# A hybrid mLSTM / short-conv block on one core: two convolutions put off into the down projection, and another split of the plain tail

## The chip, the cores and the metric

The kernel runs on one core of one Trainium2 chip. The metric is device microseconds of one execution; a time shown for a kernel is the median of its runs. PE is TensorE (the matmuls), DVE is VectorE, ACT is ScalarE, POOL is GpSimd, SP is SyncE. A name with q (ACTq, SPq) is that engine's queue of instructions that start a DMA.

## The reference, cut to what matters

512 tokens of width 2048 pass through two mixers and a gated MLP. Only the MLP and the last norm are touched:

```python
hn = rmsnorm(h, norm_ffn_g)
u = causal_dwconv(hn @ w_up, ffn_conv_w, ffn_conv_b)     # 2048 -> 2 * 5504, 3 taps over the tokens
gate, val = jnp.split(u, 2, axis=-1)
h = h + (jax.nn.silu(gate) * val) @ w_down               # 5504 -> 2048
return rmsnorm(h, norm_out_g)
```

## The kernel before, in words

Activations lie transposed: channels on the partitions, the 512 tokens on the free axis. All projections are cut into **items**. An item makes two blocks of 128 output channels for all tokens; it is worked through in **steps**, each of 512 input channels. A step has two **cells** of 21 matmuls (128x128 weights, 256 tokens): 7 products of sums of blocks in place of 8 plain ones, each as three matmuls, weight high x activation high (L281), high x low (L282), low x high (L283). For that, each step's weights are loaded into `raw` by SP (L252, L253, L262), two blocks in it are added to by accumulating DMAs of POOL (L255), sums are made by DVE (L218, L223), ACT rounds `raw` into `wh` (L233, once for each cell) and DVE takes the rest into `wl` (L237, once for each cell). There are 6 `raw`, 4 `wh` and 3 `wl` buffers. The activations of a step are made once for a phase by the same means (L344 to L354, L358, L361).

Items alternate between two sets of three PSUM banks. One of the seven products goes to a bank that both sets share (`bank_83` in the order, `P_BANK` in the code), half of it for each set; it comes first in the last cell of an item and last in every other cell. When an item's last step is issued, ACT copies its half of the shared bank into the item's buffer `z` (L305, `evac_first`), and in the next step DVE adds the other banks to it (L311 to L314, `evac_ops`). In the first and the last two items of a phase the steps of the two items alternate.

What is left to do for an item is its **post**: a list of pieces, kept in the queue `posts`, of which at most one piece each of the first two entries is issued at the end of a step. A piece is issued while `credit` (DVE time left over, counted by the program) allows it; otherwise it waits until the steps left to `due(num)` are no more than its pieces. `flush(n)` issues at once whatever posts are left up to item n. A store or add that a piece asks for is issued in the step after it (`late`).

- Up item j (items 64 to 106; `up_post`): normalise `z` (L688, DVE); two scaled copies by ACT into a buffer, mA or mB in turn (L853, L854); two taps each on DVE (L857, L858 and L861, L862); SiLU (L865, ACT); the product (L868, DVE); the store to `a_d`, which ACT issues (L150).
- Down item (items 107 to 130, three chunks of K of 8 items each; `down_post`): ACT negates half of `z` (L879), POOL adds `z` to `h_d` in DRAM by an accumulating DMA of 512 KB (L157). Chunk 0 has 3 steps to an item. Items 107 and 108 fill steps 0 to 5 of the down projection, item 109 ends at step 8, 110 at 11, 111 at 14, 112 at 17, and 113 and 114 fill steps 18 to 23.

The z of a down item is the next of a ring of five buffers (`DOWN_Z`). Before, 107 to 112 take z_93, z_92, z_91, mA, mB and again z_93, where z_93, z_92 and z_91 were the z of the up items 104, 105 and 106.

Three of the 43 input blocks of the down projection are left for the **plain part** at the end: 16 steps (n = 0 to 15; token half 0 for n below 8), 18 matmuls each (L1202 to L1204). After step n, DVE adds the partial `h` to the bank (L1215, `last_post`), ACT squares it (L1216), DVE adds the square to its half's sum (L1220, `last_acc`). A matmul with a constant sums over the partitions (L1225, `last_sum`), ACT takes the root (L1232, `last_root`), DVE makes the row that scales (L1233 to L1235). Then each (half, block pair) is scaled and written to the output: where ACT had multiplied it by the weights of the norm (L1241, `last_gain`), by one DVE product (L1248), else by two DVE operations that take in the weights (L1252); ACT issues the output DMA (L1254). SP loads the partial `h` three steps ahead (L1186, `hf_load`). Of half 0, pairs 4 to 7 have their weights from ACT, of half 1 all.

The lines that order this around the change, in the main loop:

```python
flush(it.num - 3)
evac_first(it)
...
for x in list(posts)[:2]:
    cost, fn = x[1][0]
    if not rush and cost and credit <= cost / 2 and len(x[1]) < due(x[0]) - s:
        break
    x[1].popleft()
    credit -= cost
    fn()
```

## Time and profile before

| what | value |
|---|---|
| median of 3 runs | 2601.21 us (2599.85 to 2602.29) |
| the profiled execution, its own time | 2603.19 us |
| its span, first to last instruction | 2601.5 us |
| PE busy in the span | 2548.2 us, 98% |
| DVE, ACT, POOL busy | 2123.1, 1316.3, 862.5 us |
| mean granted clock of TensorE | 0.993 of full speed |

The profiled execution's own time is 2.0 us above the median, and its span 1.7 us below its own time. Times of day below ("at 2147.64") count from the start of the span. A granted clock of 1.00 is the level of 2.4 GHz, 0.50 that of 1.2 GHz; a value between is a mean over a stretch that had both. In a timeline a row is one instruction: start, length, engine, line, operation, output<-inputs, and in brackets the idle time before it with what ended it.

### The profile page before, as it was taken

The page shows a single profiled execution, that of the slowest core. Times are in us where ns is not written, and L with a number is a line of the kernel's source. Part 1 is how long each engine was busy: PE and PEld are TensorE (multiplying, and loading weights), DVE is VectorE, ACT ScalarE, POOL GpSimd, SP SyncE. Part 2 cuts the span into 40 slices and gives each one's busy share as a digit, 9 for nine tenths or more (in the row PEclk, how much of TensorE's full clock was granted, in tenths as well). Part 3 has the DMA queues.
Part 4 walks back from the last instruction along what each step waited for, and adds up shares of the span by engine and source line. Part 5 has one row for each costly group of instructions (what it writes and reads, how often), then busy time and mean ns, then how long its engine had stood idle before and what let it go on. Part 6 is the DMA issues. An engine that isn't in the chain of part 4 may idle for free.

```text
span 2601.5 us, 55134 instructions
## 1 busy us (share of the span) xinstructions
PE 2548.2 (98%) x20886; PEld 2528.9 (97%) x20886; DVE 2123.1 (82%) x3239; ACT 1316.3 (51%) x1731; POOL 862.5 (33%) x996
## 2 busy tenths in 40 slices
PE   9999999999999999999899999999999999999997
PEld 8999999999999999999899999999999999999997
DVE  8687778886777888967889888888888898879766
ACT  7454554546556544445554544454444554545444
POOL 3343333333333212232333333333333323353430
PEclk9999999999999999999999999999999999999998
DMA  9799889898998899999989988898989889999995
GB/s 256 176 238 241 234 225 253 221 256 217 231 253 221 233 297 235 267 271 245 234 220 227 224 224 218 222 224 223 223 221 224 223 223 234 249 273 252 270 228 169
DMA packets 479003, 609.83 MB, mean 234 GB/s; under 512 B 44640, under 2 KB 309856, under 8 KB 478736
## 3 DMA queue, kind: packets, MB, share of 16 engines
q1 hardware_dynamic: 307280, 423.46, 51.5%
q0 software_dynamic: 144224, 137.67, 35.2%
q10 hardware_dynamic: 27232, 45.17, 4.8%
q8 instruction: 163, 2.67, 0.4%
q14 instruction: 104, 0.85, 0.1%
HBM read 541.65 MB, written 60.82 MB: 232 GB/s over the span
## 4 chain that ended last, share of the span: by engine, by line
PE 65%; DVE 5%; DMA 3%; issue 2%; ACT 0%; POOL 0%; DVEq 0%; SPq 0%; ACTq 0%; POOLq 0%
PE bank L283 21%; PE bank L282 21%; PE bank L281 21%; DVE act L361 1%; DVE wl L237 1%; DMA raw<-in_w_out_dram 1%; DMA raw<-in_w_up_dram 1%; DVE raw L218 0%; DMA xraw<-mc_d 0%; DMA xraw<-a_d 0%; DVE xraw L344 0%; PE bank L639 0%; DMA mc_d<-z 0%; PE bank L1204 0%; PE bank L1203 0%
## 5 line engine op out<-in xcount | busy, mean ns | idle before, releaser
L283 PE MATMUL bank<-act,wl 128*128 128x256 f32 x6712 | 1906.1, 284 | 24.3 <-DVE wl L237 23.7
L281 PE MATMUL bank<-act,wh 128*128 128x256 f32 x6712 | 1914.0, 285 | 4.9 <-ACT z L305 2.1
L282 PE MATMUL bank<-act,wh 128*128 128x256 f32 x6712 | 1903.2, 284 | 2.1 <-DVE act L361 2.1
L233 ACT ACTIVATE wh<-raw 128x896 fp32r<-128x896 f32 x904 | 858.2, 953 | 1076.1 <-PE bank L282 719.0
L283 PEld LDWEIGHTS bank<-act,wl 128*128 128x128 f32 x6712 | 1292.2, 193 | 29.2 <-DVE wl L237 29.1
L281 PEld LDWEIGHTS bank<-act,wh 128*128 128x128 f32 x6712 | 1292.2, 193 | 8.5 <-DVE z L311 2.4
L282 PEld LDWEIGHTS bank<-act,wh 128*128 128x128 f32 x6712 | 1292.2, 193 | 5.4 <-DVE act L361 2.5
L237 DVE TENSOR_TENSOR wl<-raw,wh 128x896 fp32r<-128x896 f32 x904 | 982.7, 1088 | 372.2 <-PE bank L283 244.2
L255 POOL DMA_DIRECT2D raw<-in_w_up_dram x344 | 299.2, 952 | 578.7 <-DMA raw<-in_w_up_dram 243.8
L255 POOL DMA_DIRECT2D raw<-in_w_dram x284 | 247.1, 944 | 505.2 <-DMA raw<-in_w_dram 320.9
L255 POOL DMA_DIRECT2D raw<-in_w_down_dram x160 | 141.5, 1002 | 253.0 <-DMA raw<-in_w_down_dram 144.2
L218 DVE TENSOR_TENSOR raw<-raw 128x256 f32<-128x256 f32 x452 | 189.8, 420 | 11.4 <-DMA raw<-in_w_up_dram 5.1
L223 DVE TENSOR_TENSOR raw<-raw 128x256 f32<-128x256 f32 x452 | 189.6, 420 | 0.3
L358 ACT ACTIVATE act<-xraw 128x1792 fp32r<-128x1792 f32 (+1 forms) x52 | 86.9, 1672 | 63.1 <-DVE xraw L354 61.1
L361 DVE TENSOR_TENSOR act<-xraw,act 128x1792 fp32r<-128x1792 f32 (+1 forms) x52 | 103.4, 1988 | 0.0
L688 DVE TENSOR_TENSOR z<-z,rstd 128x1024 f32<-128x1024 f32 x83 | 101.1, 1219 | 0.0
L311 DVE TENSOR_TENSOR z<-bank,z 128x512 f32<-128x512 f32 x122 | 83.6, 685 | 16.2 <-ACT z L305 12.6
L312 DVE TENSOR_TENSOR z<-bank,z 128x512 f32<-128x512 f32 x122 | 83.5, 684 | 0.8
L314 DVE TENSOR_TENSOR z<-bank,z 128x512 f32<-128x512 f32 x122 | 83.4, 684 | 0.0
L255 POOL DMA_DIRECT2D raw<-in_w_out_dram x48 | 42.9, 1019 | 105.3 <-DMA raw<-in_w_out_dram 41.2
L255 POOL DMA_DIRECT2D raw<-in_w_v_dram x32 | 38.6, 1360 | 52.1 <-DMA raw<-in_w_v_dram 32.8
L313 DVE TENSOR_TENSOR z<-bank,z 128x256 f32<-128x256 f32 x122 | 51.8, 424 | 4.2
(247 smaller groups left out, 1302.5 us busy)
## 6 DMA issues: line engine op xcount, KB each, us to landing
raw<-in_w_up_dram SPq DMA_DIRECT2D x172, 512.0 KB, 5.8
raw<-in_w_dram SPq DMA_DIRECT2D x144, 512.0 KB, 6.0
raw<-in_w_up_dram SPq DMA_DIRECT2D x344, 128.0 KB, 4.0
raw<-in_w_up_dram POOLq DMA_DIRECT2D x344, 128.0 KB, 5.5
raw<-in_w_down_dram SPq DMA_DIRECT2D x80, 512.0 KB, 6.6
raw<-in_w_dram SPq DMA_DIRECT2D x284, 128.0 KB, 4.2
raw<-in_w_dram POOLq DMA_DIRECT2D x284, 128.0 KB, 5.3
raw<-in_w_down_dram SPq DMA_DIRECT2D x160, 128.0 KB, 4.5
```

Source lines behind the costliest of these rows:

```text
L218: V.tensor_add(x[:, 6], x[:, 5], x[:, 0])
L223: V.tensor_add(x[:, 2], x[:, 6], x[:, 1])
L233: A.activation(seven(t.wh[r]), half(r), AF.Copy)
L237: V.tensor_sub(seven(t.wl[r]), half(r), seven(f(t.wh[r])))
L255: G.dma_start(at(i), a21, accum_op=ALU.add)
L281: PE.matmul(ps, h, xh, start=start, stop=False, skip_group_check=True)
L282: PE.matmul(ps, h, xl, start=False, stop=False, skip_group_check=True)
L283: PE.matmul(ps, l, xh, start=False, stop=stop, skip_group_check=True)
L311: return [lambda: V.tensor_add(z[:, 0:4:3], b0, two(z[:, 1])), lambda: V.tensor_add(z[:, 1:3], b1, two(z[:, 3])), lambda: V.tensor_add(z[: ...
L358: A.activation(t.act[:, :m], t.raw[:, :m], AF.Copy)
L361: V.tensor_sub(t.act[:, NW:NW + m], t.raw[:, :m], f(t.act[:, :m]))
L688: V.tensor_mul(sb_pair(it.z), sb_pair(it.z), two(rstd))
```

## The change

The posts of items 105 and 106, the last two up items, are held back: that of 105 until step 4 of the down projection, that of 106 until step 9 and until that of 105 is through (`put_off`). Their first scaled copy goes to mC, the second into the first half of their own z (after the taps that read it), so that mA and mB are free for the ring: 107 to 112 now take z_93, mB, mA, z_92, z_91, z_93. `due` gives the two put-off posts fixed steps and every down item the end of the item five later (before: three later). `flush` at the end of a down step reaches only items five back.

In the plain part SP issues the output DMAs, ACT applies the weights to pairs 1, 3 and 5 of half 0 (in steps 3, 5 and 7) in place of pairs 4 to 7, and a small activation in step 6 asks for the root's function table early.

```diff
--- before.py
+++ after.py
@@ -842,8 +842,9 @@
     def up_post(j):
         def post(it):
             a, b = halves(it)
+            put_off = it.num >= DOWN - 2
             buf = bufs[it.num % 2]
-            y0, y1 = buf[:, :T], buf[:, T:2 * T]
+            y0, y1 = (mC, a) if put_off else (buf[:, :T], buf[:, T:2 * T])
 
             def norm():
                 assert normal["up"]
@@ -851,11 +852,17 @@
 
             def one():
                 A.activation(y0, a, AF.Identity, scale=fwc(2, j), bias=fwc(3, j))
+                if not put_off:
+                    other()
+
+            def other():
                 A.activation(y1, b, AF.Identity, scale=fw_neg(2, j), bias=fwc(3, NF + j))
 
             def two_():
                 V.scalar_tensor_tensor(y0[:, 1:], a[:, :T - 1], fwc(1, j), y0[:, 1:], op0=ALU.mult, op1=ALU.add)
                 V.scalar_tensor_tensor(y0[:, 2:], a[:, :T - 2], fwc(0, j), y0[:, 2:], op0=ALU.mult, op1=ALU.add)
+                if put_off:
+                    other()
 
             def three():
                 V.scalar_tensor_tensor(y1[:, 1:], b[:, :T - 1], fw_neg(1, j), y1[:, 1:], op0=ALU.mult, op1=ALU.add)
@@ -885,7 +892,7 @@
     steps, items_all, all_cells = [], [], []
     DOWN = 40 + 16 + 8 + NF
     rot = [(z2, zs[1], zs[0])[(n - 40) % 3] for n in range(DOWN - 3, DOWN)]
-    DOWN_Z = rot + [b[:, :2 * T] for b in ((mA, mB) if DOWN % 2 else (mB, mA))]
+    DOWN_Z = rot[:1] + [b[:, :2 * T] for b in ((mB, mA) if DOWN % 2 else (mA, mB))] + rot[1:]
 
     def add(items, inter):
 
@@ -1251,7 +1258,7 @@
                 s = h[:, b * H2:(b + 1) * H2]
                 V.scalar_tensor_tensor(s, s, g_out(j), row, op0=ALU.mult, op1=ALU.mult)
         j1, j2 = kpair(p)
-        A.dma_start(outT[j1:j2 + 1:j2 - j1, :, half * H2:(half + 1) * H2].rearrange("j p t -> p j t"),
+        SP.dma_start(outT[j1:j2 + 1:j2 - j1, :, half * H2:(half + 1) * H2].rearrange("j p t -> p j t"),
                      h.rearrange("p (j t) -> p j t", j=2))
 
 
@@ -1373,8 +1380,16 @@
 
     def due(num):
 
+        if num >= DOWN - 2:
+            return ends.get(num + 5, len(steps)) if num >= DOWN else down_at + 9 + 5 * (num - DOWN + 2)
         n = num + 2
         return ends.get(n if n < len(items_all) and (n < 42 or items_all[n].pre) else n + 1, len(steps))
+
+    down_at = [it.num for it, q in steps[:n_main]].index(DOWN)
+
+    def put_off(num, s):
+
+        return num == DOWN - 2 and s < down_at + 4 or num == DOWN - 1 and (s < down_at + 9 or posts[0][0] < num)
 
     for s in range(START, len(steps)):
         it, q = steps[s]
@@ -1460,7 +1475,7 @@
         if main and q == it.nq - 1:
             if it.num < 42 and it.num != 2:
                 flush(it.num - 2)
-            flush(it.num - 3)
+            flush(it.num - 3 if it.num < DOWN else max(it.num - 5, DOWN - 3))
             assert it.num < 3 or getattr(items_all[it.num - 3], "z_read", True)
             evac_first(it)
             if it.pre:
@@ -1475,7 +1490,7 @@
         if s >= START + hold:
             credit = min(credit, 2.5)
             rush = not main or any(x[0] in urgent for x in posts)
-            for x in list(posts)[:2]:
+            for x in [x for x in posts if not put_off(x[0], s)][:2]:
                 if x[0] >= out_items[-1].num + 1 and not normal.get("up"):
                     break
                 cost, fn = x[1][0]
@@ -1501,11 +1516,10 @@
             for _ in range(2 if it.n < 12 else 1):
                 if finals:
                     last_scale(0, finals.popleft())
-        if not main and it.n > 7:
-            if it.n < 12:
-                last_gain(lasts[it.n - 4])
-            if it.n > 9:
-                last_gain(lasts[it.n - 2])
+        if not main and (it.n in (3, 5, 7) or it.n > 9):
+            last_gain(lasts[it.n - 2])
+        if not main and it.n == 6:
+            A.activation(sm("ny")[:, :1], eps, AF.Abs_reciprocal_sqrt)
     l, = lq
     while lsum:
         last_acc(lsum.pop())
```

Three places of the order of instructions. First, ACT at the end of items 107 and 108 (steps 4 to 6 of the down projection); L233 makes `wh`, L305 empties the shared bank. Before:

```order
L150 DMA a_d<-mA 128x512
L305 ACTIVATE z_93<-bank_83 128x256
L233 ACTIVATE wh_25885<-raw_25691 128x896
L233 ACTIVATE wh_25900<-raw_25754 128x896
L865 ACTIVATE mB<-mB 128x512
L150 DMA a_d<-mB 128x512
L305 ACTIVATE z_92<-bank_83 128x256
L233 ACTIVATE wh_25956<-raw_25754 128x896
L853 ACTIVATE mA<-z_91,pcol 128x512
L854 ACTIVATE mA<-z_91,pcol,pneg 128x512
```

Now:

```order
L150 DMA a_d<-mA 128x512
L305 ACTIVATE z_93<-bank_83 128x256
L233 ACTIVATE wh_25882<-raw_25691 128x896
L233 ACTIVATE wh_25895<-raw_25753 128x896
L305 ACTIVATE mB<-bank_83 128x256
L233 ACTIVATE wh_25946<-raw_25753 128x896
L854 ACTIVATE mC<-z_92,pcol 128x512
L233 ACTIVATE wh_25959<-raw_25759 128x896
L233 ACTIVATE wh_26009<-raw_25759 128x896
```

The scaled copies and the SiLU of item 105 and the issue of its store (`a_d<-mB`) no longer stand before the L305 of item 108; its copy into mC stands behind.

Second, ACT and POOL around the end of item 112 (step 17), which writes z_93 again. Before, the negation of item 107's z_93 on ACT stood at the end of step 10:

```order
L233 ACTIVATE wh_26264<-raw_25960 128x896
L879 ACTIVATE z_93<-z_93 128x512
L233 ACTIVATE wh_26277<-raw_26024 128x896
L305 ACTIVATE mA<-bank_83 128x256
L233 ACTIVATE wh_26325<-raw_26024 128x896
```

Now it stands at the end of step 16, and the next step's L305 writes the same buffer:

```order
L233 ACTIVATE wh_26619<-raw_26320 128x896
L886 ACTIVATE z_93<-z_93 128x512
L886 ACTIVATE mB<-mB 128x512
L233 ACTIVATE wh_26633<-raw_26385 128x896
L305 ACTIVATE z_93<-bank_83 128x256
L233 ACTIVATE wh_26682<-raw_26385 128x896
L886 ACTIVATE mA<-mA 128x512
L886 ACTIVATE z_92<-z_92 128x512
```

On POOL, the add of z_93 to `h_d` and the loads around it; `raw_26623` holds the weights of step 22:

```order
L255 DMA raw_26504<-in_w_down_dram 128x256 x2
L255 DMA raw_26623<-in_w_down_dram 128x256 x2
L157 DMA h_d<-z_93 128x2x512
L157 DMA h_d<-mB 128x2x512
L255 DMA raw_26686<-in_w_down_dram 128x256 x2
L157 DMA h_d<-mA 128x2x512
L157 DMA h_d<-z_92 128x2x512
```

The row L305 z_93 writes what the DMA in L157 z_93 reads, and has to wait for it to land; before, six whole steps (11 to 16) lay between the negation and this L305, now none.

Third, ACT in the plain part, around the root of half 0 (L1232 before, L1239 now). L1216 and L1223 are the squares, L1241 and L1248 the weights. Before:

```order
L1216 ACTIVATE z_93<-hf_30520 128x512
L1216 ACTIVATE z_92<-hf_30627 128x512
L1241 ACTIVATE hf_30520<-hf_30520,pcol 128x256 x2
L1216 ACTIVATE mB<-hf_30627 128x512
L1232 ACT_TABLE_LOAD
L1232 ACTIVATE rstd<-bank_85,rs_106 128x256
L1241 ACTIVATE hf_30520<-hf_30520,pcol 128x256 x2
L1216 ACTIVATE mB<-hf_30627 128x512
L1254 DMA out_dram<-hf_30520 128x2x256 x2
L1241 ACTIVATE hf_30520<-hf_30520,pcol 128x256 x2
L1241 ACTIVATE hf_30627<-hf_30627,pcol 128x256 x2
L1216 ACTIVATE z_93<-hf_30627 128x512
```

Now:

```order
L1223 ACTIVATE z_91<-hf_30520 128x512
L1522 ACT_TABLE_LOAD
L1522 ACTIVATE ny<-rs_106 128x1
L1223 ACTIVATE z_93<-hf_30520 128x512
L1248 ACTIVATE hf_30520<-hf_30520,pcol 128x256 x2
L1223 ACTIVATE mB<-hf_30629 128x512
L1223 ACTIVATE z_91<-hf_30629 128x512
L1239 ACTIVATE rstd<-bank_85,rs_106 128x256
L1223 ACTIVATE z_91<-hf_30629 128x512
L1248 ACTIVATE hf_30629<-hf_30629,pcol 128x256 x2
L1223 ACTIVATE z_93<-hf_30629 128x512
```

The table load stands between the squares of steps 5 and 6 and not before the root, and no output DMA stands between squares and weights.

## Rows read from the trace of the kernel before

**Rows 1.** The page's first part: busy time, share of the span and instructions of each engine.

```profile
PE 2548.2 (98%) x20886; PEld 2528.9 (97%) x20886; DVE 2123.1 (82%) x3239; ACT 1316.3 (51%) x1731; POOL 862.5 (33%) x996
```

**Rows 2.** Busy time by stretch: the stretch and its length, busy time (and instructions) of PE, PEld, DVE, ACT and POOL, the granted clock, the DMA share and GB/s. The first is a steady stretch of the up projection, the next three lie in the switch from up to down, the last in the plain part's end.

```profile
1300.00:1500.00 200.00, 200.00 (x1669) 200.00 (x1669) 177.69 (x261) 100.80 (x123) 69.88 (x82) 1.00 0.90 223
2120.00:2130.00 10.00, 7.17 (x59) 6.77 (x57) 9.93 (x16) 5.21 (x6) 3.49 (x4) 1.00 0.93 242
2140.00:2150.00 10.00, 7.96 (x57) 7.55 (x56) 9.96 (x14) 5.03 (x7) 5.24 (x6) 0.90 1.05 293
2160.00:2170.00 10.00, 7.92 (x54) 7.72 (x53) 9.30 (x16) 4.43 (x6) 2.54 (x3) 0.83 0.80 179
2580.00:2590.00 10.00, 5.31 (x20) 3.56 (x19) 6.35 (x11) 7.00 (x15) 0.00 (x0) 0.75 0.25 87
```

**Rows 3.** PE's timeline in the switch: the matmuls that waited, and the first and the last of a run of 16 that follow one another without a wait (row 4 and row 5).

```profile
2123.12 0.38 PE L283 MATMUL bank<-act,wl 128*128 128x256 f32 x1 [1.26 <-DVE wl L237]
...
2129.98 0.38 PE L283 MATMUL bank<-act,wl 128*128 128x256 f32 x1 [1.57 <-DVE wl L237]
...
2147.64 0.39 PE L283 MATMUL bank<-act,wl 128*128 128x256 f32 x1 [1.90 <-DVE wl L237]
...
2148.17 0.42 PE L283 MATMUL bank<-act,wl 128*128 128x256 f32 x1
...
2151.37 0.30 PE L283 MATMUL bank<-act,wl 128*128 128x256 f32 x1
...
2163.48 0.39 PE L281 MATMUL bank<-act,wh 128*128 128x256 f32 x1 [2.08 <-ACT z L305]
```

**Rows 4.** DVE's timeline in the switch.

```profile
2145.03 1.22 DVE L688 TENSOR_TENSOR z<-z,rstd 128x1024 f32<-128x1024 f32 x1
2146.16 0.42 DVE L218 TENSOR_TENSOR raw<-raw 128x256 f32<-128x256 f32 x1
...
2152.80 0.75 DVE L857 SCALAR_TENSOR_TENSOR mB<-z,pcol,mB 128x511 f32<-128x511 f32 x1
...
2154.24 1.22 DVE L688 TENSOR_TENSOR z<-z,rstd 128x1024 f32<-128x1024 f32 x1
...
2161.94 0.69 DVE L868 TENSOR_TENSOR mB<-mB 128x512 f32<-128x512 f32 x1
```

**Rows 5.** ACT's timeline at the end of item 108; ACTq is the issue of a DMA.

```profile
2157.75 0.61 ACT L865 ACTIVATE mB<-mB 128x512 f32<-128x512 f32 x1
2162.67 0.33 ACTq L150 DMA_DIRECT2D a_d<-mB  x1
2163.04 0.38 ACT L305 ACTIVATE z<-bank 128x256 f32<-128x256 f32 x1 [4.67 <-DVE raw L218]
```

**Rows 6.** SP's timeline: the first load of a step's weights. The second row belongs to the weights of step 22.

```profile
2202.10 0.33 SPq L252 DMA_DIRECT2D raw<-in_w_down_dram  x1
...
2217.22 0.33 SPq L252 DMA_DIRECT2D raw<-in_w_down_dram  x1
```

**Rows 7.** POOL's timeline: the accumulating DMAs for the weights that the first row of rows 6 begins, an add to `h_d` behind them, and the second of the two accumulating DMAs for the weights of step 22.

```profile
2205.95 1.78 POOL L255 DMA_DIRECT2D raw<-in_w_down_dram  x2 [2.33 <-DMA raw<-in_w_down_dram]
2207.74 1.22 POOL L157 DMA_DIRECT2D h_d<-z  x1
...
2226.40 0.87 POOL L255 DMA_DIRECT2D raw<-in_w_down_dram  x1 [0.79 <-DMA raw<-in_w_down_dram]
```

**Rows 8.** ACT's timeline: the `wh` that had waited for the end of step 16 of the down projection.

```profile
2218.49 0.96 ACT L233 ACTIVATE wh<-raw 128x896 fp32r<-128x896 f32 x1 [1.58 <-PE bank L282]
```

**Rows 9.** The adds by L157, all 28 of the program: time from issue to landing; then the issues of two short stretches of chunk 0 (from 2207 and from 2216): KB each, median us from issue to landing.

```profile
DMA to landing us min/median/max: 5.8/9.8/15.3
...
h_d<-z POOLq DMA_DIRECT2D x1, 512.0 KB, 9.0
...
h_d<-mB POOLq DMA_DIRECT2D x1, 512.0 KB, 12.8
```

**Rows 10.** DMA issues of the last 100 us: the loads of the partial `h` (count, KB each, median us to landing).

```profile
hf<-h_d SPq DMA_DIRECT2D x16, 256.0 KB, 5.3
```

**Rows 11.** ACT's timeline in the plain part: a square with the idle time before it, the table load and the root of half 0, the last square, the root of half 1.

```profile
2562.81 0.63 ACT L1216 ACTIVATE z<-hf 128x512 f32<-128x512 f32 x1 [1.41 <-DVE hf L1215]
...
2568.55 1.28 ACT L1232 ACT_TABLE_LOAD   x1 [1.08 <-PE bank L1225]
2569.85 0.47 ACT L1232 ACTIVATE rstd<-bank,rs 128x256 f32<-128x256 f32 x1
...
2587.33 0.61 ACT L1216 ACTIVATE z<-hf 128x512 f32<-128x512 f32 x1
...
2590.11 0.47 ACT L1232 ACTIVATE rstd<-bank,rs 128x256 f32<-128x256 f32 x1 [1.23 <-PE bank L1225]
```

**Rows 12.** DVE's timeline in the plain part: the add of step 9, four scalings with weights, one scaling without, the add of step 15.

```profile
2571.62 0.68 DVE L1215 TENSOR_TENSOR hf<-bank,hf 128x512 f32<-128x512 f32 x1
2572.22 1.66 DVE L1252 SCALAR_TENSOR_TENSOR hf<-hf,pcol,rstd 128x256 f32<-128x256 f32 x4
...
2577.84 0.68 DVE L1248 TENSOR_TENSOR hf<-hf,rstd 128x512 f32<-128x512 f32 x1
...
2585.97 0.68 DVE L1215 TENSOR_TENSOR hf<-bank,hf 128x512 f32<-128x512 f32 x1
```

**Rows 13.** PE's timeline: the first four matmuls of the last sum, before the root of half 1.

```profile
2586.11 2.08 PE L1225 MATMUL bank<-mB,identw 128*128 128x256 f32 x4 [4.69 <-DVE mB L1220]
```

## The prediction

> **What bounds the kernel.** I read the page's busy shares first: PE is busy 98% of the span [rows 1], so the kernel is a stream of matmuls, and only what makes PE wait or run slowly can be won. In a steady stretch 1669 matmuls take 200 us, 0.12 us each, so a cell of 21 takes 2.52 us and a step 5.04 us; the granted clock there is 1.00 and DVE is busy 89% [rows 2]. Then I looked for stretches in which PE falls short. The change touches two of them: the switch from the up to the down projection, and the end of the plain part.
>
> In the switch DVE is busy over 99% in the first two stretches and PE is not [rows 2]: it waits 1.26, 1.57 and 1.90 us for a `wl` that DVE makes, and at 2163.48 2.08 us for the copy of the shared bank by ACT [rows 3]. After the last two of these waits the clock falls too: at 2148.17 to 2151.37 PE needs 3.20 us for 15 matmuls, 0.213 us each in place of 0.12, and the stretches' granted clock is 0.90 and 0.83, while it stayed at 1.00 behind the waits of 1.26 and 1.57 us [rows 2, 3]. So a spell at the lower level (1.2 GHz) costs 3.20 - 15 x 0.12 = 1.4 us, 1.5 with its edges.
>
> The wait at 2163.48 is no want of ACT time. ACT stands at the issue of the store of item 105, which needs DVE's product that begins at 2161.94 and is done at 2162.6; the issue runs at 2162.67, and behind it L305 at 2163.04 [rows 4, 5]. PE met it 18 matmuls into step 6, at the first one that writes the shared bank.
>
> In the plain part the chain runs through DVE: its add of step 9 is at 2571.62, after the root of half 0, and from there it is late to the end; the add of step 15 runs at 2585.97, though PE had that step ready at 2581.4 [rows 12, 13] (before its sum at 2586.11 PE idles 4.69 us).
>
> **The switch, term by term.** The rows ahead of item 105's normalisation (L688 at 2145.03) don't change in order, so the waits of 1.26 and 1.57 us stay. That L688 lies before the `wl` that PE waited for until 2147.64; it held DVE 2146.16 - 2145.03 = 1.13 us [rows 4], and now comes later. The wait of 1.90 becomes 0.8 us: 1.1 us won. A wait of 0.8 is shorter than those that left the clock alone, so I count its low spell as gone: 1.5 us. The two taps at 2152.80 (1.44 us to the next L688) and the rest of item 105's post leave the steps up to 6, no store stands before L305 of item 108, and the wait of 2.08 us goes, with its low spell of 1.5 us. Together 1.1 + 1.5 + 2.1 + 1.5 = **6.2 us**; at the least 3.2, if both spells stay.
>
> What is put off is some 10 us of DVE (two normalisations of 1.13, four pairs of taps of 1.44, two products of 0.6), now in steps 4 to 13 of the down projection. A down step asks DVE for 2.7 us of weights, and 2.3 us more after an item's end; from the step after item 108's end on, nine steps come to 39 us with the put-off work, in 45 us of PE. It fits, and the first copies into mC wait for nothing that is late: nothing for this, and if it doesn't quite fit, up to 2 us.
>
> **What is late next.** The change's `due` lets an add to `h_d` wait for the end of the item five later, and the order shows that it does so for item 107: its z_93 is negated at the end of step 16, its add is issued in step 17, and the L305 of item 112 in step 17 writes z_93 again. Step 16 ends at 2218.49 in the trace of before [rows 8]; I count from there. Without the wait PE would need that L305 at 5.04 + 18 x 0.12 = 7.2 us, as in step 6. On POOL the add stands behind the accumulating DMAs for the weights of step 22, whose load SP starts at 2217.22, that is at -1.27 [rows 6]. Such DMAs began 2205.95 - 2202.10 = 3.85 us after their load and took 1.78 us [rows 6, 7], so the add is issued at -1.27 + 3.85 + 1.78 = 4.4. An add right behind them, at 2207.74, landed after 9.0 us [rows 7, 9]: 13.4, and with L305 (0.38) PE goes on at 13.8. It waits 13.8 - 7.2 = 6.6 us, and a low spell follows, since 6.6 is far over the 1.90 that was enough: **8.1 us lost**. From below: the add at 1.4 (behind one `wh` of 0.96 and two halves of 0.5), landing after the shortest time, 5.8 us: 7.6, so 0.4 us. From above: the accumulating DMAs for step 22 were through only at 2226.40 + 0.87, that is at 8.8, with adds before them that the change moves away; with the 12.8 us of the slowest add there, PE goes on at 22.0 and loses 14.8 + 1.5 = 16.3 us. I take 8.1, from the rows of the same phase without a crowd. DVE, which waits for the same L305, is back with a `wl` 3 us later, when PE has 3 us of work left. The other down items get their buffer back three steps or more after the add, and cost nothing. Four more adds now fall just before chunk 1; I price that at nothing, and at 4 us from above.
>
> **The plain part.** The table load (1.28 us) stands between the end of PE's sum and the root; without it the root starts at 2568.55 and not at 2569.85, 1.30 us sooner [rows 11]. Its new place is an idle time of 1.41 us before a square [rows 11], so it delays nothing there.
>
> The Trainium skill (ScalarE: Activation LUTs, What ACT_TABLE_LOAD costs) puts a switch of tables at 1.28 us and a drain of 1.38 us, 2.66 together. By that the new place would not do, the old one would give back 2.66, and the sum would come out about 1.3 us lower. The trace has the root 20 ns behind the load [rows 11], and so no drain there.
>
> From the root on, DVE's time between the adds of step 9 and step 15 is 5 adds more (0.60 each, and that of step 9), 6 sums (0.61), five pairs with weights (half of 1.58, 0.79) and three without (0.72): 3.6 + 3.7 + 4.0 + 2.2 = 13.4 us, against 2585.97 - 2571.62 = 14.35 before [rows 12]. Before, DVE also waited for squares that stood behind output issues and weights on ACT; now SP issues the outputs, and ACT has 0.6 + 0.85 us to do in a step of over 2. The add of step 15 comes at 2570.3 + 13.4 = 2583.7, 2.3 us sooner. The last sum's eight matmuls take 2.08 us for four [rows 13], at a granted clock that was 0.75 in this stretch [rows 2]; PE's idle time before them shrinks from 4.7 to 2.4 us, which is still over 1.90, so I leave them slow. The root of half 1 comes at 2583.75 + 4.16 = 2587.9 in place of 2590.11 [rows 11], and all behind it is as before: **2.2 us**, at least 1, and up to 4 if the clock holds. The loads of `h` for steps 14 and 15 now stand on SP behind output DMAs; they go out at about 2573 and 2576 and land 5.3 us later [rows 10], 2 to 3 us before their adds: nothing.
>
> **Sum.** -6.2 + 8.1 - 2.2 = -0.3 us. The sum stands against the profiled execution's own 2603.2 us, which gives 2602.9; the runs' median lies 2.0 us lower, so I forecast **2601 us**. A measurement of this kernel can tell a change from none at about 0.2%, 5.2 us.
>
> **Rivals.**
> 1. The add lands in time, or PE doesn't meet L305 so soon: 6.2 + 2.2 are won, 2601.2 - 8.4 = 2592.8 us. For it: the shortest landing of 5.8 us. Against: it asks for POOL to be free when the negation ends, and the order puts two accumulating DMAs first. The gain passes 5.2 us where the wait costs under 3.2. 17%.
> 2. Slower: POOL and the DMA queue hold the add back as they held the weights of step 22 before (8.8 us), and PE loses 16.3 us: 2601.2 - 8.4 + 16.3 = 2609.1 us. Slower by more than can be told from no change where the wait costs over 13.6 us, so where PE goes on later than at 19.3 in place of 13.8. Against: the adds of items 108 to 111 no longer crowd that stretch. 13%.
> 3. The table load holds ACT for as long again as its own row; then moving it gives 1.3 us more, 2599.7 us. Against: the 20 ns of rows 11. 2%. (The Trainium skill, ScalarE: Activation LUTs, has it so.)
> 4. The tail gives nothing, since the loads of `h` behind the outputs come late: 2603 us. 5%.
>
> The forecast itself has 63%. Faster by over 0.2%: rival 1 and a little of the forecast's lower end, 0.20. Slower: rival 2 and a little more for the crowd at chunk 1, 0.16. Same: 0.64. The range goes from rival 1 to rival 2, 2593 to 2609.
>
> **What would show it.** Right: in the switch only the waits of 1.26 and 1.57 us and one near 0.8; none on L305 at the end of item 108; then, at about 2220, one PE wait on L305 in step 18 of several us, with ACT waiting for a DMA of z_93 before it; the table load between two squares; the root of half 1 some 19.4 us behind that of half 0 (2590.11 - 2569.85 = 20.3 before). Wrong: no PE wait in step 18, or one over 12 us; a wait in steps 6 to 13 for a `wl`, with DVE at 99% there; a DVE wait for `hf` in steps 14 and 15.

## The result, and the profile after

The changed kernel takes 2606.7 us (median of 11 runs, 2602.7 to 2609.3), the kernel before 2601.1 (11 runs): a ratio of 1.0017, with a 95% interval of 1.0010 to 1.0025, so 2.6 to 6.5 us slower. Timed again (e10 below), the ratio was 1.0015 (1.0006 to 1.0024). The forecast was 2601 us, no change that can be measured. The time lies inside the stated range, but the difference can be told from nothing, and it is a loss where the sum had a gain of 0.3 us.

The profiled execution's own time is 2606.7 us, its span 2605.0. In the listings below, code behind line 853 stands 7 lines further down than before: the negation L879 is L886, the square L1216 is L1223, the last sum L1225 is L1232, the root L1232 is L1239.

The page's first part answers to [rows 1]; it tells of no difference, PE has 1.0 us less to do and a longer span:

```profile
span 2605.0 us, 55136 instructions
PE 2547.2 (98%) x20886; PEld 2527.4 (97%) x20886; DVE 2122.2 (81%) x3240; ACT 1314.8 (50%) x1730; POOL 862.9 (33%) x996
```

**The switch.** PE's timeline, the matmuls that waited, answers to [rows 3]:

```profile
2124.97 0.39 PE L283 MATMUL bank<-act,wl 128*128 128x256 f32 x1 [1.26 <-DVE wl L237]
...
2131.83 0.39 PE L283 MATMUL bank<-act,wl 128*128 128x256 f32 x1 [1.56 <-DVE wl L237]
...
2148.36 0.39 PE L283 MATMUL bank<-act,wl 128*128 128x256 f32 x1 [0.76 <-DVE wl L237]
```

1.26, 1.56 and 0.76 us as forecast, and no wait on L305. Busy time by stretch (columns as in [rows 2]), of the switch and of the stretches behind the two waits that follow:

```profile
2140.00:2160.00 20.00, 19.11 (x158) 18.71 (x157) 19.90 (x31) 10.79 (x13) 8.96 (x11) 1.00 1.08 299
2226.00:2232.00 6.00, 5.08 (x24) 5.08 (x25) 5.06 (x8) 3.10 (x5) 2.21 (x2) 0.50 0.79 127
2255.00:2261.00 6.00, 5.04 (x29) 5.04 (x30) 5.97 (x9) 3.75 (x5) 2.13 (x3) 0.72 0.98 252
```

In the switch the clock is 1.00 though DVE is at 99%; the two other rows, at 0.50 and 0.72, are where it is lost.

**The stall.** ACT's timeline at the end of steps 16 and 17, then PE's, then POOL's to the start of chunk 1:

```profile
2214.72 0.62 ACT L886 ACTIVATE z<-z 128x512 f32<-128x512 f32 x1
...
2226.49 0.38 ACT L305 ACTIVATE z<-bank 128x256 f32<-128x256 f32 x1 [9.15 <-DMA h_d<-z]
```

```profile
2226.92 0.58 PE L281 MATMUL bank<-act,wh 128*128 128x256 f32 x1 [5.83 <-ACT z L305]
```

```profile
2216.95 1.56 POOL L157 DMA_DIRECT2D h_d<-z  x1
2217.67 2.08 POOL L157 DMA_DIRECT2D h_d<-mB  x1
...
2229.78 1.21 POOL L157 DMA_DIRECT2D h_d<-mA  x1 [3.93 <-ACT wh L233]
2230.51 1.73 POOL L157 DMA_DIRECT2D h_d<-z  x1
2235.66 2.42 POOL L157 DMA_DIRECT2D h_d<-z  x2 [3.43 <-ACT z L886]
```

The negation of z_93 ends at 2215.3, the add is issued at 2216.95, ACT stands 9.15 us for its landing before L305 at 2226.49, and PE waits 5.83 us. The clock behind it is 0.50 (1.2 GHz) to 2232. POOL's other rows are the adds of items 108 to 112: four of them go out between 2229.78 and 2238.

**Chunk 1.** There DVE waits for activations that SP loads from `a_d`, and PE for DVE. DVE's row and PE's in the changed kernel, and then in the kernel before at the same place:

```profile
2251.14 0.69 DVE L344 TENSOR_TENSOR xraw<-xraw 128x512 f32<-128x512 f32 x1 [4.96 <-DMA xraw<-a_d]
```

```profile
2255.96 0.45 PE L283 MATMUL bank<-act,wl 128*128 128x256 f32 x1 [3.18 <-DVE wl L237]
```

```profile
2244.60 0.69 DVE L344 TENSOR_TENSOR xraw<-xraw 128x512 f32<-128x512 f32 x1 [2.21 <-DMA xraw<-a_d]
```

```profile
2257.42 0.58 PE L283 MATMUL bank<-act,wl 128*128 128x256 f32 x1 [1.89 <-DVE wl L237]
```

DVE waits 4.96 us in place of 2.21. The load was issued at 2238.07 (before: 2234.27). Its two halves, by the answer for that line and time, first in the changed kernel, then in the kernel before:

```profile
DMA to landing us min/median/max: 11.6/12.1/12.6
```

```profile
DMA to landing us min/median/max: 8.8/9.3/9.9
```

**The tail.** ACT's rows around the table load and the two roots, and DVE's add of step 15, answer to [rows 11, 12]:

```profile
2567.05 1.28 ACT L1522 ACT_TABLE_LOAD   x1
2568.34 0.20 ACT L1522 ACTIVATE ny<-rs 128x1 f32<-128x1 f32 x1
2568.45 0.62 ACT L1223 ACTIVATE z<-hf 128x512 f32<-128x512 f32 x1
...
2575.04 0.47 ACT L1239 ACTIVATE rstd<-bank,rs 128x256 f32<-128x256 f32 x1 [1.66 <-PE bank L1232]
...
2593.60 0.47 ACT L1239 ACTIVATE rstd<-bank,rs 128x256 f32<-128x256 f32 x1 [1.23 <-PE bank L1232]
```

```profile
2589.96 0.68 DVE L1222 TENSOR_TENSOR hf<-bank,hf 128x512 f32<-128x512 f32 x1
```

The unchanged matmuls before the plain part run 6.52 us later than in the trace of before; by that measure the root of half 0 is 1.33 us sooner, the add of step 15 2.53 and the root of half 1 3.03 us sooner.

**How traces are compared here.** Before the switch, where the code is the same, the copy L305 of item 105 starts between 2111.9 and 2119.9 us in the twelve traces of this study: spans differ by up to 8 us before any edit acts. So I compare intervals between copies L305: from item 106 to 110 (the switch, 69.4 us before), from 110 to 114 (step 17 and the start of chunk 1, 64.9), from 114 to 130 (the rest of the down projection, 287.4), and from there to the end (57.6). The table gives the difference to the first trace of before, in us, and the measured ratio.

| kernel | 106 to 110 | 110 to 114 | 114 to 130 | to the end | ratio to before (95%) |
|---|---|---|---|---|---|
| before, again (e8) | -2.0 | -1.3 | 0.0 | 0.0 | |
| tail only (e1) | -2.2 | -0.1 | 0.0 | -3.0 | 0.9991 (0.9983 to 1.0000) |
| before, adds late (e7) | -1.8 | +4.5 | +3.0 | 0.0 | 1.0013 (1.0004 to 1.0022) |
| changed | -6.5 | +11.2 | 0.0 | -3.0 | 1.0017 (1.0010 to 1.0025) |
| changed, again (e10) | -6.5 | +11.4 | +1.9 | -4.0 | 1.0015 (1.0006 to 1.0024) |
| switch only (e2) | -6.5 | +11.0 | +2.5 | 0.0 | 1.0033 (1.0021 to 1.0046) |
| 107 early (e3) | -6.5 | +3.1 | +1.8 | -2.8 | 0.9990 (0.9981 to 0.9999) |
| all adds three later (e4) | -6.5 | +3.3 | +0.3 | -3.5 | 0.9984 (0.9975 to 0.9992) |
| adds at once (e5) | -6.5 | +0.1 | +2.9 | -3.0 | 0.9977 (0.9967 to 0.9986) |
| four adds left out (e6) | -6.5 | -2.3 | +0.1 | -2.8 | |
| adds in a turn of their own (e9) | -6.5 | -2.3 | +0.9 | -4.0 | 0.9956 (0.9944 to 0.9969) |

### The profile page after: what moved, and what is told of

Same layout as the page of the kernel before. It is cut to its first block, busy times and chain, and to the rows that moved or that the text cites. A ratio compares the mean times of both kernels' runs of the same rounds, so it can differ in the third digit from the quotient of the medians.

```text
span 2605.0 us, 55136 instructions
## 1 busy us (share of the span) xinstructions
PE 2547.2 (98%) x20886; PEld 2527.4 (97%) x20886; DVE 2122.2 (81%) x3240; ACT 1314.8 (50%) x1730; POOL 862.9 (33%) x996
## 4 chain that ended last, share of the span: by engine, by line
PE 68%; DVE 5%; DMA 2%; issue 1%; ACT 0%; POOL 0%; DVEq 0%; POOLq 0%; ACTq 0%; SPq 0%
PE bank L283 22%; PE bank L282 22%; PE bank L281 22%; DVE act L361 1%; DVE wl L237 1%; DMA raw<-in_w_out_dram 1%; DMA xraw<-a_d 0%; PE bank L1210 0%; PE bank L1211 0%; PE bank L1209 0%; DVE raw L218 0%; DMA h_d<-z 0%; DVE xraw L344 0%; PE bank L639 0%; DVE raw L223 0%
## 5 line engine op out<-in xcount | busy, mean ns | idle before, releaser
L233 ACT ACTIVATE wh<-raw 128x896 fp32r<-128x896 f32 x904 | 857.7, 953 | 1076.7 <-PE bank L282 711.4
L255 POOL DMA_DIRECT2D raw<-in_w_v_dram x32 | 38.6, 1360 | 51.1 <-DMA raw<-in_w_v_dram 30.7
L305 ACT ACTIVATE z<-bank 128x256 f32<-128x256 f32 x121 | 44.3, 366 | 21.1 <-PE bank L283 11.5
```

Source lines behind the costliest of these rows:

```text
L233: A.activation(seven(t.wh[r]), half(r), AF.Copy)
L255: G.dma_start(at(i), a21, accum_op=ALU.add)
```

## The experiments

### The two halves apart: e1 and e2

e1 is the kernel before with the plain part's edits alone:

```diff
-        A.dma_start(outT[j1:j2 + 1:j2 - j1, :, half * H2:(half + 1) * H2].rearrange("j p t -> p j t"),
+        SP.dma_start(outT[j1:j2 + 1:j2 - j1, :, half * H2:(half + 1) * H2].rearrange("j p t -> p j t"),
...
-        if not main and it.n > 7:
-            if it.n < 12:
-                last_gain(lasts[it.n - 4])
-            if it.n > 9:
-                last_gain(lasts[it.n - 2])
+        if not main and (it.n in (3, 5, 7) or it.n > 9):
+            last_gain(lasts[it.n - 2])
+        if not main and it.n == 6:
+            A.activation(sm("ny")[:, :1], eps, AF.Abs_reciprocal_sqrt)
```

> The kernel before with the plain part of the change alone (outputs by SyncE, weights on ScalarE for pairs 1, 3, 5, the root's table asked for in step 6). My theory, that the tail gains what the profile of the changed kernel shows there: 2.2 to 3.0 us less than before, a ratio near 0.999. The rival, that the trace of one execution flatters the tail and a part of the loss comes from it: no gain, a ratio of 1.000 or above. The order of instructions ahead of the plain part is that of before, so the waits in the switch (1.26, 1.57, 1.90 and 2.08 us) must be there again.

Measured: 0.9991 (0.9983 to 1.0000), 2.3 us less; 3.0 us in the trace. The tail gains what it was to gain, though the interval of the times just reaches to no gain.

e2 is the changed kernel with these lines as before.

> The changed kernel with the plain part as before. My theory, from the profile of the changed kernel: the switch gains 6.5 us, the wait for item 107's add and its low spell lose about 8, the stretch before chunk 1 loses about 3: slower than before by some 4.6 us, a ratio near 1.0018. By the terms of the prediction (6.2 won, 8.1 lost, nothing at chunk 1) it would be 1.9 us slower, 1.0007. The rival, that the changed kernel is slow for a reason spread over code that the change does not touch: the waits read from the trace explain less than the time measured, by 2 to 4 us.

Measured: 1.0033, 8.6 us slower (5.5 to 12.0). It is more than my 4.6; 2.5 us of the rest stand in the trace behind item 114, where PE waited 0.59, 0.55 and 1.89 us at the start of chunk 2. With these, and against the usual switch of before (e8, below), the trace explains 9 us, so nothing need be left that is spread over other code. So the loss lies in the part that moves convolutions and adds. e1 and e2 together give 6.3 us where the change gave 4.4; the intervals allow it.

### Which adds cost what: e3 and e4

Both are the changed kernel with another `due` for down items; the second piece is e4.

```diff
-            return ends.get(num + 5, len(steps)) if num >= DOWN else down_at + 9 + 5 * (num - DOWN + 2)
+            return ends.get(num + (3 if num == DOWN else 5), len(steps)) if num >= DOWN else down_at + 9 + 5 * (num - DOWN + 2)
```

```diff
-            return ends.get(num + 5, len(steps)) if num >= DOWN else down_at + 9 + 5 * (num - DOWN + 2)
+            return ends.get(num + 3, len(steps)) if num >= DOWN else down_at + 9 + 5 * (num - DOWN + 2)
```

> The changed kernel with one number changed: the add of item 107 alone is due at the end of item 110 (three later), those of the others stay at five later. The wait of PE for L305 in step 18 (5.83 us) must go. Theory A, two causes (the late add, and apart from it the four adds 108 to 111 that crowd the DMAs for chunk 1): about 8 us faster than the changed kernel and 3.6 us faster than before (ratio near 0.9986), and the wait of some 3 us near 2253 stays. Theory B, one cause (the stall in step 18 throws the loads for chunk 1 out of step, the adds don't matter): 11 us faster than the changed kernel, 6.6 faster than before (ratio 0.9975), and the wait near 2253 shrinks to the 0.4 to 1.9 us of before.

> The changed kernel with the adds of all down items due at the end of the item three later, as before; what is put off stays put off. Theory A and theory B both: neither the wait in step 18 nor the longer one at chunk 1, 11.1 us faster than the changed kernel, 6.6 faster than before (ratio 0.9975), and by the terms of the trace alone (6.5 in the switch, 3.0 in the tail) up to 9.5 faster (0.9963). Theory A has it 3 us faster than the run with item 107 alone early, theory B the same as that run. If put-off DVE work needed the room that the late adds gave, a wait for a wl shows in steps 6 to 16.

Measured: e3 0.9990, 2.6 us faster than before; e4 0.9984, 4.2 us faster. In both the wait for L305 in step 18 is gone, and between items 110 and 114 some 8 us come back of 11.2. The other 3 us stay in both. That fells theory B: there is no stall any more that could throw chunk 1 out of step, and PE still waits 3.5 us there. It looked to fell theory A as well, since e4 gives all adds the `due` of before. DVE's row of e4 at chunk 1, PE's, and POOL's before them:

```profile
2240.82 0.69 DVE L344 TENSOR_TENSOR xraw<-xraw 128x512 f32<-128x512 f32 x1 [5.54 <-DMA xraw<-a_d]
```

```profile
2245.64 0.58 PE L283 MATMUL bank<-act,wl 128*128 128x256 f32 x1 [3.76 <-DVE wl L237]
```

```profile
2215.44 1.91 POOL L157 DMA_DIRECT2D h_d<-mA  x1
2217.12 1.47 POOL L157 DMA_DIRECT2D h_d<-z  x1
...
2222.00 1.56 POOL L157 DMA_DIRECT2D h_d<-z  x1
2224.81 1.21 POOL L157 DMA_DIRECT2D h_d<-z  x1 [1.25 <-ACT z L886]
```

POOL's rows show that e4 did not do what I meant. The four rows are the adds of items 109 to 112. Counted from the L305 of item 110, those of 109, 110 and 111 went out 8.5, 9.5 and 12.6 us later than in the kernel before. They were not queued behind the put-off posts, as what I expected of e5 below has it: the store of item 106, which follows its last piece, was issued at 2198.79, three steps before the add of 109. What held them was `credit`, which the put-off posts had used up. By the program's count it was still below zero at the end of steps 14 and 15, where the kernel before had enough for the adds of 109 and 110 (step 14) and of 111 (step 15); so in e4 they waited for `due` and `credit` until steps 16 and 17. Three adds went out from 2217.12 on, shortly before the load of 2227.16, and landed while it was under way; it took 12.3 to 13.2 us to land. In the kernel before, one add (at 2231.92) began in the 10 us before that load. Hence a third theory beside A: C, the load takes that long whenever PE is there earlier.

### The crowd of adds by itself: e6 and e7

e6 is e4 without four adds:

```diff
-                add_to(pair_ap(h_d, j1, j2), sb_pair(it.z), ("d", c, p))
+                if DOWN + 2 <= it.num <= DOWN + 5:
+                    stored.add(("d", c, p))
+                else:
+                    add_to(pair_ap(h_d, j1, j2), sb_pair(it.z), ("d", c, p))
```

> As the run with all adds due three later, but the four adds to h_d of items 109 to 112 are left out (these eight blocks of the output lack their first third of the down projection). It is for its trace alone. Theory A: the load of a_d lands in under 10 us and the wait of 3.76 us at chunk 1 goes below 1.9 us. Theory C: landing 13 us, the wait stays.

The load of 2229.39 lands after 3.9 us, PE's wait of 3.76 us becomes one of 1.09, and DVE, here at chunk 1, waits for nothing:

```profile
2243.43 0.69 DVE L344 TENSOR_TENSOR xraw<-xraw 128x512 f32<-128x512 f32 x1
```

The interval from 110 to 114 is 5.6 us shorter than in e4 (-2.3 against +3.3). Theory C falls. The share of the DMA engines by queue in 22 us before DVE's L344 (packets, MB, share of 16 engines; the software queue is POOL's, the hardware queue SP's and ACT's), in the changed kernel from 2229 to 2251 and in e6 from 2220 to 2242:

```profile
q0 software_dynamic: 1461, 2.43, 67.0%
q1 hardware_dynamic: 1526, 2.33, 32.1%
```

```profile
q1 hardware_dynamic: 2543, 3.93, 52.8%
q0 software_dynamic: 894, 0.81, 27.6%
```

In the changed kernel POOL's queue moves as many bytes as SP's and takes twice the engines' time; without the four adds its share falls from 67% to 28%. The Trainium skill (DMA: Bandwidth & Descriptors, Queues, rings and completion order) says that a DMA engine serves the queues that have work for it in turn, a packet at a time. The landing times go with that, 12.6 us beside four adds and 3.9 beside none; that the packets alternate no row here shows.

e7 makes the same test from the other side: the kernel before, with the adds of items 109 to 111 held back.

```diff
+    down_at = [it.num for it, q in steps[:n_main]].index(DOWN)
...
-            flush(it.num - 3)
+            flush(it.num - 3 if not 112 <= it.num <= 114 else 108)
...
-            for x in list(posts)[:2]:
+            for x in [x for x in posts if not (x[0] in (109, 110) and s < down_at + 18 or x[0] == 111 and s < down_at + 19)][:2]:
```

> The kernel before with the adds of items 109 to 111 held until steps 18 and 19 of the down projection, as late as in the changed kernel; nothing else is changed, and no buffer is needed sooner than the add is through. Theory A: the load of a_d for chunk 1 lands after 12 us or more in place of 9.9, PE waits about 3 us there in place of 0.6 and 1.9, and the kernel is 2 to 3 us slower than before, ratio near 1.001. Theory C: no difference.

Measured: 1.0013 (1.0004 to 1.0022), 3.4 us slower, and 4.5 us lost between items 110 and 114. Three of POOL's four adds, then the waits of DVE and of PE:

```profile
2228.68 1.21 POOL L157 DMA_DIRECT2D h_d<-z  x1 [4.57 <-ACT wh L233]
...
2231.68 2.52 POOL L157 DMA_DIRECT2D h_d<-mB  x1
2232.41 3.03 POOL L157 DMA_DIRECT2D h_d<-z  x1
```

```profile
2249.25 0.69 DVE L344 TENSOR_TENSOR xraw<-xraw 128x512 f32<-128x512 f32 x1 [2.47 <-DMA xraw<-a_d]
```

```profile
2255.21 0.58 PE L281 MATMUL bank<-act,wh 128*128 128x256 f32 x1 [4.67 <-DVE z L311]
```

The mechanism is as in theory A, though not the very load, since the adds of 109 to 111 came a step later here than in the changed kernel: the load at 2229.77 landed after 8.7 us, and the next, at 2237.91, after 10.9, with the wait behind it. So late adds alone, without any put-off work, cost some 3 us. The trace shows more, since 3.0 us are lost behind item 114 as well, at the start of chunk 2; whether those are the adds' no run tells.

### Adds early: e5 and e9

e5 is e4 with the adds ahead of the put-off posts and due one item later:

```diff
-            return ends.get(num + 3, len(steps)) if num >= DOWN else down_at + 9 + 5 * (num - DOWN + 2)
+            return ends.get(num + 1, len(steps)) if num >= DOWN else down_at + 9 + 5 * (num - DOWN + 2)
...
-            for x in [x for x in posts if not put_off(x[0], s)][:2]:
+            for x in sorted([x for x in posts if not put_off(x[0], s)], key=lambda x: x[0] < DOWN)[:2]:
```

> The changed kernel with the adds of down items issued in the steps right behind their item (their posts go ahead of the put-off ones and are due one item later). The run with all adds due three later still waited 3.76 us for a wl at chunk 1, because its adds, queued behind the put-off posts, still began 11.7, 10.0, 5.2 and 2.4 us before the load of a_d that DVE waited for (before: one at 2.4, the others 18 us or more). Theory A, the adds crowd that load: now at most one add within 10 us of it, DVE waits 2.2 us or less for it, PE at most 1.9 us, and the kernel is about 3 us faster than the run with all due three later: some 7 us under before, ratio 0.997. Theory C, the load of a_d takes 13 us whenever PE arrives there earlier, whatever the adds do: the waits of 5.5 us (DVE) and 3.8 us (PE) stay, ratio 0.998.

Measured: 0.9977, 6.0 us faster than before. DVE no longer waits for the load of 2225.71 (landing 7.3 us), as theory A has it. But two new waits, 4.2 us together, took back a good part of what was won; ACT's and PE's rows at the end of item 111:

```profile
2200.91 0.33 ACTq L150 DMA_DIRECT2D a_d<-mC  x1
2201.33 0.38 ACT L305 ACTIVATE z<-bank 128x256 f32<-128x256 f32 x1 [2.30 <-DVE raw L218]
```

```profile
2201.77 0.39 PE L281 MATMUL bank<-act,wh 128*128 128x256 f32 x1 [2.14 <-ACT z L305]
```

It is the wait of [rows 5] again, for another item. The adds, now ahead of the put-off posts, held up their pieces, so that item 106's product on DVE began only at 2200.18, 1.2 us before L305 (4.3 us before it in the changed kernel); its store (L150), which stands before L305 on ACT in both, waited for it. The other wait, 2.02 us for a `wl` at 2271.21, follows an add at 2253.27 in the first steps of chunk 1: SP's loads of weights right behind that add landed after 6.5 to 8.3 us, and after 2.0 to 4.6 in e9 below, where no add is there.

e9 is the changed kernel with a turn of their own for the adds, and with the first steps of chunk 1 free of them:

```diff
-            return ends.get(num + 5, len(steps)) if num >= DOWN else down_at + 9 + 5 * (num - DOWN + 2)
+            return ends.get(num + (1 if num < DOWN + 5 else 5), len(steps)) if num >= DOWN else down_at + 9 + 5 * (num - DOWN + 2)
...
-            for x in [x for x in posts if not put_off(x[0], s)][:2]:
+            ready = [x for x in posts if not put_off(x[0], s)]
+            for group in [x for x in ready if x[0] < DOWN][:2], [x for x in ready if x[0] >= DOWN][:1 if main else 2]:
+                for x in group:
```

> The changed kernel with a turn of their own for the adds of down items: in each step up to one, beside the pieces of the put-off posts, due one item later for items 107 to 111 and five later for the others. In the run with adds at once, these took the place of a piece of item 106's post, whose store then stood before the copy of the shared bank of item 111 (PE waited 2.14 us at 2201.77), and an add of a chunk-1 item crowded the weights of the next step (2.02 us at 2271.21). Here DVE's order is that of the changed kernel, five adds land before the loads for chunk 1 begin, and no more follow until the first steps of chunk 1 are through. Expected: no wait on a copy of the shared bank, at chunk 1 only the waits of 1.1 and 1.6 us; against before 4.4 us from the switch, some 2 from chunk 1, 3 from the tail: 8 to 10 us faster, a ratio of 0.996 to 0.997, and 4 us faster than the run with adds at once. If the crowd isn't what costs at chunk 1, or adds beside the weights of steps 9 to 16 cost as much: no faster than that run (0.9977).

Measured: 2590.1 us, a ratio of 0.9956 (0.9944 to 0.9969) to before, 11.4 us faster, somewhat more than I expected; it beats both kernels. Between the switch and the end of chunk 1's first steps PE has two waits; they, and four of POOL's six adds, are:

```profile
2246.84 0.39 PE L283 MATMUL bank<-act,wl 128*128 128x256 f32 x1 [1.09 <-DVE wl L237]
...
2253.71 0.39 PE L283 MATMUL bank<-act,wl 128*128 128x256 f32 x1 [1.56 <-DVE wl L237]
```

```profile
2160.88 1.91 POOL L157 DMA_DIRECT2D h_d<-z  x1
...
2172.98 1.56 POOL L157 DMA_DIRECT2D h_d<-mB  x1
...
2217.01 1.56 POOL L157 DMA_DIRECT2D h_d<-z  x1
...
2223.65 1.21 POOL L157 DMA_DIRECT2D h_d<-z  x1 [3.25 <-ACT z L886]
```

The six adds of items 107 to 112 are spread over 63 us. Two of them still begin in the 10 us before the load of 2226.00, which lands after 7.3 us.

### Both kernels again: e8 and e10

> The kernel before, unchanged, for a second trace of it. In the first trace a stretch of low clock followed the waits of 1.90 and 2.08 us in the switch; in the run with the tail alone, whose switch has the same order, PE waited 1.90 and 1.42 us and only the first had one. If the switch of before costs between 4.3 and 6.5 us more than that of the changed kernel from one execution to another, the trace that I predicted from had the long form, and the gain in the switch is counted too high by up to 2 us. Expected: 4 to 6.5 us between the same two copies of the shared bank.

> The changed kernel, unchanged, on the same chip as the one above, for a second ratio and a second trace. Expected: slower than before by 4 us again (ratio 1.001 to 1.0025), with the wait for L305 in step 18 (5 to 7 us with a spell of low clock, together 8 to 9 us) and some 3 us at chunk 1. If one of the two does not come again, it belonged to that execution.

e10 came out as expected (PE waits 5.67 us for L305 and 3.35 us at chunk 1). e8 shows that the trace I predicted from was not the usual one in the switch. PE's waits and the stretches behind them in e8 (the stretch, busy time and instructions of PE, the clock, the DMA share, GB/s), and then the stretch behind the wait for L305 in the first trace of before:

```profile
2147.12 0.38 PE L283 MATMUL bank<-act,wl 128*128 128x256 f32 x1 [1.89 <-DVE wl L237]
...
2162.43 0.39 PE L281 MATMUL bank<-act,wh 128*128 128x256 f32 x1 [1.57 <-ACT z L305]
```

```profile
2147.00:2153.00 6.00, 5.88 (x36) 0.72 1.05 296
2161.00:2167.00 6.00, 4.57 (x38) 1.00 0.91 223
```

```profile
2162.00:2168.00 6.00, 4.52 (x27) 0.76 0.88 213
```

Behind the wait of 1.9 us for a `wl` the clock falls in e8 (0.72) as it did in the first trace [rows 3]. Behind the wait for L305 it fell only in the first trace (0.76), where that wait was 2.08 us; in e8, e1 and e7 it was 1.57, 1.42 and 1.75, the clock stayed at 1.00, and the switch took 2.0, 2.2 and 1.8 us less.

## Why the prediction was right or wrong

- **Switch, 6.2 us.** The mechanism is right in each part: the waits are those named. Against the trace it was worked out from, it gained 6.5 us, in every kernel that has it. Against the four traces of that code in this study (0, -2.0, -2.2, -1.8, a mean of -1.5) it gained 5.0. I took the second spell of low clock, and the last 0.5 us of the wait before it, for a fixed cost of that code; it was one execution's. Nor does a wait's length alone tell of a spell, as I had it: e5 waited 2.14 us for L305 and kept its clock at 1.00.
- **Put-off work fits, 0.** Right: DVE is at 99% to 2180, and no wait appears in steps 6 to 16.
- **The stall, 8.1 us.** Right in mechanism; the size came out by errors that cancel. From L305 of item 110 to SP's load of 2238.07 the changed kernel takes 8.4 us longer than before (51.1 against 42.7), 8.5 in e10, 8.9 in e2. The add went out 3.1 us into step 17 and not 4.4, the wait was 5.8 and not 6.6; the low clock behind it cost some 2.6 us and not 1.5. The shortest landing of 5.8 us, in the bound from below and in rival 1, was not of such an add: the line of [rows 9] has 30 and not 28, six of them add to another tensor, and its shortest is one of those six. Of the 24 adds to `h_d` in that trace the shortest took 7.2 us, so the bound was 1.4 us too low.
- **Chunk 1: this step failed.** The prediction put it so: "Four more adds now fall just before chunk 1; I price that at nothing, and at 4 us from above." No reason stood beside the nothing. It cost 11.16 - 8.42 = 2.7 us (2.9 in e10, 2.1 in e2), and 3.1 and 3.3 us where the stall was gone (e3, e4). e6 and e7 show that it was the adds: leave four out, and DVE's wait for the load goes; hold three back in the kernel before, and 3.4 us are lost. A warning was in the trace of before: DVE waited 2.2 us for that load even there (1.0 in e8), with a single add in the 10 us ahead of it.
- **Plain part, 2.2 us.** The root of half 0 came 1.33 us sooner (forecast 1.30), the add of step 15 2.53 (2.3), the root of half 1 3.03 (2.2), since the last sum began at the full clock (granted 1.00 for its first 0.5 us; in the kernel before it had 0.50 throughout). The runs give 2.3 us (0 to 4.4).
- **The table load at double cost.** The Trainium skill (ScalarE: Activation LUTs, What ACT_TABLE_LOAD costs) adds a drain of 1.38 us to the load. In its new place the next activation starts 10 ns behind the load's 1.28 us, and the root gained 1.33 us, not 2.66: no drain at either place.

With these sizes the sum is -5.0 + 8.4 + 2.7 + 0.5 - 3.0 = +3.6 us; the 0.5 is there because before, e1 and e8 stand at 0, -0.1 and -1.3 at chunk 1, a mean of -0.5. Measured: +4.4 and +3.9. The call of no change rested on a sum of -0.3 that two terms, 1.2 us in the switch and 3 us at chunk 1, made wrong in the same direction. None of the rivals is what happened: the wait for L305 was neither avoided (1) nor long (2), and the tail gave its gain (4). Open is the start of chunk 2: 1.9 and 2.5 us were lost there in e10 and e2, and 1.8 and 3.0 in e3 and e7, each with a wait of 1.89 us and a spell of low clock; none in the first trace of the changed kernel, and no run takes it apart.

What would have decided for a gain was in the change's own order: the put-off posts use up `credit`, so the adds wait until `due` lets them go, and the change sets that five items later. With the adds early and in a turn of their own (e9) the same moves win 11.4 us.

## What to carry to other kernels

When work is put off in a queue, list what shares the queue and its budget and so comes late too, and ask of each how soon its buffer is written again and what transfer its DMA then runs beside. A transfer that an engine already waits for has no room: price every large DMA moved next to it, by the wait that is there. Before a wait or a clock spell of one trace goes into a sum, see whether it would be there the next time: a cost of 2 us that comes and goes is as large as the difference in question.

## What the runs showed of the hardware

- The second half (256 KB) of the load from DRAM that the L344 shown above needs at the start of chunk 1 landed in 3.9 us with no accumulating DMA of 512 KB begun in the 10 us before it (e6), in 7.3 to 9.9 with one or two (before, e1, e5, e7, e8, e9), and in 12.0 to 13.2 with two to four (changed, e10, e2 to e4). The order is not strict: e4 had two and the longest time, and the next load of e7 had four and took 10.9.
- A byte in POOL's queue, which holds the accumulating DMAs, took the engines at least twice the time of one in SP's: 2.43 MB for 67% against 2.33 MB for 32% of the same 22 us, and in e6 0.81 MB for 28% against 3.93 MB for 53%.
- The length of a wait did not tell whether PE's clock fell behind it. Behind 1.89 or 1.90 us in the switch of before it fell in all four traces (0.72 over 6 us), behind 1.89 us in e9 (2372.31), and 2.02 and 2.14 us in e5, it stayed at 1.00. Such a spell cost some 1.4 to 1.5 us, that behind the stall of 5.8 us some 2.6.
